# Average pooling on one core: stores of two tiles in one 4 MiB DMA, the first one held back

## The chip, the cores and the metric

One core of one Trainium2 chip. The time is device microseconds (us) of that core; lower is better.

## The reference

```python
def setup_inputs():
    return {"x": np.random.randn(64, 256, 8192).astype(np.float32),
            "kernel_size": 4, "stride": 4}

def reference(x, kernel_size, stride):
    # output[:, :, i] = mean(x[:, :, 4*i : 4*i+4]), shape (64, 256, 2048)
    ...
```

Each output is the mean of four neighbours. 536.87 MB are read, 134.22 MB written, and every output costs three additions and one multiplication. Moving the data is the work.

## The kernel before

The 64 x 256 = 16384 rows are cut into 64 tiles of 256 rows: 128 partitions with two rows each. A tile's load is 8 MiB, 64 KiB of contiguous HBM in each partition; its store is 2 MiB, 16 KiB in each partition. There are two input buffers (`_NIN`) and four output buffers (`_NOUT`). The SP queue loads, DVE adds neighbours in two passes (8.7 and 4.4 us), ACT multiplies by 1/4 (3.6 us) and issues the store. A load waits until the second pass on the tile two before it is done.

```python
_NIN, _NOUT = 2, 4
U, E = _NOUT, NT // _NOUT - 1            # NT = 64 tiles

def load(h, u, r0=0, r1=R, wait=True):
    b = u % _NIN
    if wait:
        nc.sync.wait_ge(s_dve, h * U + (u - _NIN + 1))
    nc.sync.dma_start(
        out=xin[:, b * T + r0 * L : b * T + r1 * L],
        in_=xg[:, h * U + u, r0 * L : r1 * L],
    ).then_inc(s_last if r0 > 0 else s_in[b], 16)

def add_up(h, u, r0=0, r1=R):            # on DVE
    ...                                  # waits: output buffer stored, tile landed
    pairs(half, src).then_inc(s_half, 1)
    ...
    pairs(obuf(u, r0, r1), half).then_inc(s_dve, 1)

# ... ACT, the steady loop:
with nc.scalar.Fori(0, E) as h:
    for u in range(1, U + 1):
        v = u % U
        nc.scalar.wait_ge(s_dve, h * U + (u + 1))
        nc.scalar.mul(obuf(v), obuf(v), inv_k).then_inc(s_act, 1)
        nc.scalar.wait_ge(s_act, h * U + (u + 1))
        nc.scalar.dma_start(out=og[:, h * U + u, :], in_=obuf(v)).then_inc(s_out[v], 16)
# ... the last tiles are stored from the SP queue, the very last in two halves
```

## Time and profile before

| | before |
|---|---|
| time, median of the 3 runs given with it | 1554.84 us (1554.72 to 1555.09) |
| span in the profile | 1553.0 us |
| moved | 671.1 MB, 432 GB/s over the span |
| DMA engines' time in packets | 80.8% + 19.2% = 100% |
| DVE, ACT busy | 54%, 15% |
| period of a tile in the middle | 24.18 us |

The page of the kernel before. Its queue lines give packets, megabytes and the share of 16 engines' span that the packets took (q1 is the SP queue, with all loads and the last stores; q10 is the ACT queue, with the other stores). The group line of DVE ends with the idle time before it and what ended it. The issue lines give KB of one DMA and the median time from issue to landing.

```profile
span 1553.0 us, 976 instructions
...
DMA packets 18720, 671.10 MB, mean 432 GB/s; under 512 B 2080, under 2 KB 2080, under 8 KB 2080
...
q1 hardware_dynamic: 9936, 543.17, 80.8%
q10 hardware_dynamic: 8784, 127.93, 19.2%
...
L85 DVE TENSOR_TENSOR xin<-xin 128x8192 f32<-128x8192 f32 (+1 forms) x65 | 556.5, 8561 | 702.3 <-DMA xin<-in_x_dram 702.3
...
out_dram<-res ACTq DMA_DIRECT2D x61, 2048.0 KB, 52.4
...
xin<-in_x_dram SPq DMA_DIRECT2D x63, 35.0
```

The two shares add up to the whole span: apart from about 2 us at the start and 1.5 us at the end, no engine of the 16 has free time. (Recorded durations overlap by 3 to 4 ns from one packet to the next, 2418 ns recorded against 2414 from start to start, which is why the sum reaches 100% in spite of the two ends.) DVE waits 702 us for loads and for nothing else. A store lands 52.4 us after its issue although a new one is issued every 24.2 us, so there is always a second store queued behind the one in progress.

The windows view of two tile periods (columns: the stretch, its length, busy time of DVE, ACT and POOL, the granted clock, the DMA share, GB/s):

```profile
300.00:348.36 48.36, 26.23 (x4) 7.23 (x2) 0.00 (x0) 1.00 1.00 434
```

Two tiles are 20 MiB; 20 MiB in 48.36 us is 434 GB/s at a DMA share of 1.00. The Trainium skill ("DMA: Bandwidth & Descriptors", section "Where 436 GB/s comes from") puts the ceiling of a core's DMA fabric at 435 GB/s; this trace agrees, and loads and stores share it. The same section expects transfers between HBM and SBUF to be held to about 358 GB/s by the HBM side; with one core at work that was not so here, and the measured 434 GB/s decides.

The packet records of one engine, listed from the trace (time, queue, bytes, recorded duration in ns; records of 4 bytes are a DMA's completion). The engine's identity is not recorded: this is one chain in which each record starts where another ends. First the middle of the run, then the first store of the run:

```
400082  q10  16384   611          53612  q1   65536  2418
400689  q1       4     9          56026  q1   65536  2441
400695  q10  16384   611          58464  q1   65536  3249   <- slow
401302  q1   65536  2418          61710  q10  16384   611   <- first store
403716  q10  16384   611          62317  q1       4     9
404323  q1   65536  2418          62323  q10  16384   611
406738  q10  16384   611          62930  q1   65536  2418
```

Left: strict turns between the two queues, and a completion record uses a turn, though it takes only 6 ns. Right: beside the first store a load packet takes 0.83 us longer than the usual 2.418. Added over all 16 engines and divided by 16, this is the **excess**: 0.89 us between 50 and 95 us, and 0.00 from 100 us to the end. Only records that are more than 12 ns over the usual duration of their size are counted.

### The profile page before, as it was taken

To read this page: it belongs to the slowest core of one execution; us is meant where nothing else is said; L and a number is where in the kernel's file an instruction comes from. 1 tells how busy PE (TensorE), PEld (TensorE's weight loads), DVE (VectorE), ACT (ScalarE), POOL (GpSimd) and SP (SyncE) were. 2 spreads that over 40 slices of the span, in tenths; PEclk is the share of its full clock that TensorE was granted. 3 is DMA by queue.
4 is the path that set the end of the run, shared out by engine and by line. 5 is a ranking of instruction groups with operands and counts; after the bars stand their busy time and mean duration, and the time that the engine had idled before them with its cause. 6 is when DMAs were issued, how large, how long until landed. Compare 5 with 4: busy or idle time off the path is not lost.

```text
span 1553.0 us, 976 instructions
## 1 busy us (share of the span) xinstructions
DVE 839.8 (54%) x130; ACT 232.9 (15%) x66; POOL 0.2 (0%) x4
## 2 busy tenths in 40 slices
DVE  3645546456465564654646546455464554645546
ACT  1111011110111101101011010110101101111011
POOL 0000000000000000000000000000000000000000
DMA  9999999999999999999999999999999999999999
GB/s 405 425 433 439 439 439 436 415 439 432 439 439 439 432 417 434 439 439 432 442 415 433 438 432 446 439 420 428 434 440 439 439 432 418 433 439 439 439 425 405
DMA packets 18720, 671.10 MB, mean 432 GB/s; under 512 B 2080, under 2 KB 2080, under 8 KB 2080
## 3 DMA queue, kind: packets, MB, share of 16 engines
q1 hardware_dynamic: 9936, 543.17, 80.8%
q10 hardware_dynamic: 8784, 127.93, 19.2%
HBM read 536.87 MB, written 134.22 MB: 432 GB/s over the span
## 4 chain that ended last, share of the span: by engine, by line
DMA 72%; DVE 27%; issue 0%; SPq 0%; ACT 0%; DVEq 0%
DMA xin<-in_x_dram 72%; DVE xin L85 18%; DVE res L85 9%; SPq L68 0%; ACT res L106 0%; DVEq L96 0%; SPq L188 0%; SPq L57 0%
## 5 line engine op out<-in xcount | busy, mean ns | idle before, releaser
L85 DVE TENSOR_TENSOR xin<-xin 128x8192 f32<-128x8192 f32 (+1 forms) x65 | 556.5, 8561 | 702.3 <-DMA xin<-in_x_dram 702.3
L141 ACT ACTIVATE res<-res 128x4096 f32<-128x4096 f32 x60 | 217.0, 3616 | 1225.8 <-DVE res L85 1225.8
L85 DVE TENSOR_TENSOR res<-xin 128x4096 f32<-128x4096 f32 (+1 forms) x65 | 283.4, 4359 | 2.2
L106 ACT ACTIVATE res<-res 128x4096 f32<-128x4096 f32 (+1 forms) x5 | 14.7, 2933 | 86.6 <-DVE res L85 86.6
L106 ACT ACT_TABLE_LOAD x1 | 1.3, 1283 | 0.9 <-SPq L57 0.9
L174 POOL MEMSET const-bfloat16-1.0<- 128x1 bf16 x1 | 0.1, 101 | 0.0
L174 POOL MEMSET const-uint8-127<- 128x1 uint8 x1 | 0.1, 101 | 0.0
L174 POOL MEMSET const-float32-0.0<- 128x1 f32 x1 | 0.1, 98 | 0.2 <-issue 0.2
L174 POOL MEMSET const-float32-1.0<- 128x1 f32 x1 | 0.1, 98 | 0.0
## 6 DMA issues: line engine op xcount, KB each, us to landing
out_dram<-res ACTq DMA_DIRECT2D x61, 2048.0 KB, 52.4
xin<-in_x_dram SPq DMA_DIRECT2D x2, 4096.0 KB, 29.5
out_dram<-res SPq DMA_DIRECT2D x2, 2048.0 KB, 26.1
out_dram<-res SPq DMA_DIRECT2D x2, 1024.0 KB, 9.4
xin<-in_x_dram SPq DMA_DIRECT2D x63, 35.0
```

Source lines behind the costliest of these rows:

```text
L85: return nc.vector.tensor_tensor(out=out, in0=v[:, :, 0], in1=v[:, :, 1], op=mybir.AluOpType.add)
L106: nc.scalar.mul(o, o, inv_k).then_inc(s_act, 1)
L141: nc.scalar.mul(obuf(v), obuf(v), inv_k).then_inc(s_act, 1)
L174: nc = _bacc.Bacc("TRN2", target_bir_lowering=False, num_devices=1)
```

## The change

The intent, as stated: one 4 MiB store for every two tiles, still in 16 KiB packets, so that half as many stores are issued; the first store is held until the third tile has landed, so that the next one is queued in time. The output memory stays the same: two buffers of two tiles instead of four of one.

```diff
+_G = 2
-_NOUT = 4
+_NOUT = 2
+    og2 = of.rearrange("(g t p r) m -> p g t (r m)", t=G, p=P, r=R)
-    res = pool.tile([P, _NOUT * OT], dt)
+    res = pool.tile([P, _NOUT * G * OT], dt)
@@ the store
-            eng.dma_start(
-                out=og[:, h * U + u, : r1 * OL], in_=obuf(u, 0, r1)
-            ).then_inc(s_out[u], 16)
+            eng.dma_start(
+                out=og2[:, h * _NOUT + u // G, :, :],
+                in_=res[:, (u + 1 - G) * OT : (u + 1) * OT].rearrange(
+                    "p (t m) -> p t m", t=G
+                ),
+            ).then_inc(s_out[u // G], 16)
@@ DVE waits for a stored output buffer after its first pass, not before it
-                nc.vector.wait_ge(s_out[u], h * 16)
             pairs(half, src).then_inc(s_half, 1)
+            if u % G == 0:
+                nc.vector.wait_ge(s_out[u // G], h * 16)
@@ ACT: the hold, and a store after every second tile
-        scale(0, 0)
-        nc.scalar.wait_ge(s_dve, 2)
-        store(nc.scalar, 0, 0)
+        for u in range(G):
+            scale(0, u)
+        nc.scalar.wait_ge(s_in[0], 32)
+        store(nc.scalar, 0, G - 1)
     # (the steady loop issues one store where u % G == G - 1;
     #  the last stores, 4 + 2 + 1 + 1 MiB, go out from the SP queue. Cut.)
```

More of the change, by code (lines that the diff above doesn't have):

```diff
@@ L36 @@
     R = _R
+    G = _G
     T, OT = R * L, R * OL
-    assert OL * K == L and rows % (P * R * _NOUT) == 0
+    assert OL * K == L and rows % (P * R * G * _NOUT) == 0
     NT = rows // (P * R)
@@ L57 @@
     with tc.tile_critical():
-        U = _NOUT
+        U = _NOUT * G
         E = NT // U - 1
@@ L74, in obuf, with store, store_rows @@
             return res[:, u * OT + r0 * OL : u * OT + r1 * OL]
-        def store(eng, h, u, r1=R):
-            eng.wait_ge(s_act, h * U + (u + (1 if r1 == R else r1)))
+        def store(eng, h, u):
+            eng.wait_ge(s_act, h * U + (u + 1))
             eng.dma_start(
-                out=og[:, h * U + u, : r1 * OL], in_=obuf(u, 0, r1)
-            ).then_inc(s_out[u], 16)
+                out=og2[:, h * _NOUT + u // G, :, :],
[3 more added lines that the diff above has]
+            ).then_inc(s_out[u // G], 16)
+        def store_rows(eng, u, r1, scaled):
+            eng.wait_ge(s_act, scaled)
+            eng.dma_start(
+                out=og[:, E * U + u, : r1 * OL], in_=obuf(u, 0, r1)
+            ).then_inc(s_in[0], 16)
         def pairs(out, src):
@@ L118 @@
             load(E, U - 1, r, r + 1, wait=r == 0)
-        for u in range(1, U - 1):
-            store(nc.sync, E, u)
-        store(nc.sync, E, U - 1, R - 1)
+        store(nc.sync, E, G - 1)
+        store_rows(nc.sync, U - 2, R, NT - 1)
+        store_rows(nc.sync, U - 1, R - 1, NT - 1 + R - 1)
         with nc.vector.Fori(0, E) as h:
@@ L130 @@
             add_up(E, U - 1, r, r + 1)
-        scale(0, 0)
-        nc.scalar.wait_ge(s_dve, 2)
-        store(nc.scalar, 0, 0)
-        with nc.scalar.Fori(0, E) as h:
-            for u in range(1, U + 1):
+        for u in range(G):
+            scale(0, u)
+        nc.scalar.wait_ge(s_in[0], 32)
+        store(nc.scalar, 0, G - 1)
+        with nc.scalar.Fori(0, E - 1) as h:
+            for u in range(G, U + G):
                 v = u % U
@@ L141 @@
                 nc.scalar.mul(obuf(v), obuf(v), inv_k).then_inc(s_act, 1)
-                nc.scalar.wait_ge(s_act, h * U + (u + 1))
-                nc.scalar.dma_start(out=og[:, h * U + u, :], in_=obuf(v)).then_inc(
-                    s_out[v], 16
-                )
-        scale(E, 1)
-        scale(E, 2)
-        scale(E, 3, 0, 1)
-        scale(E, 3, 1, 2)
-        nc.sync.wait_ge(s_out[0], E * 16 + 16)
+                if u % G == G - 1:
+                    nc.scalar.wait_ge(s_act, h * U + (u + 1))
+                    nc.scalar.dma_start(
+                        out=og2[:, h * _NOUT + u // G, :, :],
+                        in_=res[:, (v + 1 - G) * OT : (v + 1) * OT].rearrange(
+                            "p (t m) -> p t m", t=G
+                        ),
+                    ).then_inc(s_out[v // G], 16)
+        for u in range(G, U):
+            scale(E - 1, u)
+        store(nc.scalar, E - 1, U - 1)
+        for u in range(U - 1):
+            scale(E, u)
+        for r in range(R):
+            scale(E, U - 1, r, r + 1)
+        nc.sync.wait_ge(s_out[1], E * 16)
     nc.sync.dma_start(
-        out=og[:, NT - 1, (R - 1) * OL :], in_=res[:, _NOUT * OT - OL :]
+        out=og[:, NT - 1, (R - 1) * OL :], in_=res[:, _NOUT * G * OT - OL :]
     )
```

## The prediction

> **What bounds the kernel now.** The DMA engines: the page's queue table gives 80.8% + 19.2% = 100% of 16 engines' span; 671.1 MB in 1553.0 us is 432 GB/s. DVE is busy 54%, ACT 15%. The windows view of two tiles (100 to 148.36 us) gives DMA share 1.00. In the packet records an engine passes a 64 KiB load packet every 2.414 us when loads run alone, and a load packet plus a 16 KiB store packet every 3.022 us when both queues have work: alternating costs nothing. Eight such pairs and two completion records (6 ns each) make a tile's 24.18 us. All engines are idle only for some 2 us at the start and 1.5 at the end. So at most about 3 us (0.2%) can be won.
>
> **What the change does.** Bytes, packet sizes (stores were in 16 KiB packets already), loads, DVE and ACT work stay. About 32 completion records per engine go: 0.2 us. The last DVE, ACT and store steps stay hidden behind queued stores. Issues (0.34 us on ACT) are off the path. In work alone the change is worth 0 to 0.3 us.
>
> **The queue's turns.** In the records each engine alternates strictly between load and store queue, and a completion record takes a turn like a packet. (The Trainium skill, "DMA: Bandwidth & Descriptors", section "Queues, rings and completion order", says that each engine round-robins between queues at packet granularity; this trace agrees.) Before, a tile takes 8+1 load turns and a store 8+1: balanced, so the store queue, once filled, never empties. After, two tiles take 18 load turns, one 4 MiB store 16+1 = 17: the store queue runs ahead by one turn, about 2.2 us, per pair. A store is ready about 19 us after its second tile lands (DVE 8.7+4.4, ACT 3.6, issue, start-up). Holding the first store gives the second about 5 us of margin; after three or four stores it is used up, and from then on the store queue empties before each next store, some 26 times.
>
> An empty store queue alone costs nothing, since loads fill the time. But the one time that stores started beside running loads in the before kernel (about 58 us), the packets then in flight took 3.2 to 3.4 us instead of 2.42 on all 16 engines: 0.9 us lost. If each restart costs that, 26 x 0.9 = 23 us: about 1578. If it is paid only the first time, about 1554.7. I hold the recurring stall for somewhat more likely (about 60%), given that the queue empties at all (about 85%).
>
> **Prediction.** 1570 us, between the two outcomes and nearer the slower; 8 in 10 between 1553.5 and 1581. Faster by over 2%: 1%. Within 2%: 95%. Slower by over 2%: 4%.
>
> **What would show it.** A period of 48.36 us per two tiles: no stall; near 49.3, with 64 KiB packets of about 3.3 us once per two tiles: the stall recurs. The store queue's packets should pause once per store from about the fifth store on. DVE waits for loads alone; a wait on output buffers before its second addition would be new and is not expected (about 19 us of margin). Last load to end: 14 to 20 us, without idle engines.
>
> **What would make it wrong.** A 4 MiB store's completion taking more turns, so that the queue never empties (1554.7); a stall of another size; rows 2 MiB apart per partition written slower than 0.607 us a packet; an idle end, if the last stores queue worse than worked out.

## The result, and the profile after

| | before | after |
|---|---|---|
| time, median of 4 runs | 1554.91 us | 1554.91 us |
| range | 1554.72 to 1555.09 | 1554.75 to 1555.18 |
| ratio, 95% interval | | 1.0000 (0.9983 to 1.0018) |
| span | 1553.0 us | 1553.0 us |
| last packet ends | 1551.8 us | 1551.7 us |
| completion records per engine | 130 | 99 |

Ratios, here and below, are the mean time of one kernel's fast runs over that of the other's of the same rounds, so not quite the ratio of the medians that are quoted.

The page of the kernel after; the lines answer to those of before:

```profile
span 1553.0 us, 843 instructions
...
DMA packets 18224, 671.09 MB, mean 432 GB/s; under 512 B 1584, under 2 KB 1584, under 8 KB 1584
...
q1 hardware_dynamic: 10064, 545.26, 81.1%
q10 hardware_dynamic: 8160, 125.83, 18.9%
...
L100 DVE TENSOR_TENSOR xin<-xin 128x8192 f32<-128x8192 f32 (+1 forms) x65 | 556.4, 8561 | 697.8 <-DMA xin<-in_x_dram 697.8
...
out_dram<-res ACTq DMA_DIRECT2D x30, 4096.0 KB, 49.5
...
xin<-in_x_dram SPq DMA_DIRECT2D x63, 35.0
```

The same shares, the same waits of DVE. The packet count fell by 496 = 31 x 16 completion records. At about 5.8 ns each that is 31 x 5.8 ns = 0.18 us per engine, which is all that the change removes. The windows view of the same stretch after the change:

```profile
300.00:348.36 48.36, 26.23 (x4) 7.23 (x2) 0.00 (x0) 1.00 1.00 434
```

The line is the same to the last digit. The store queue, however, does what the prediction worked out. One engine's records around the end of one store and the start of the next, after the change:

```
295472  q10  16384   611
296079  q1   65536  2418
298498  q10      4     9   <- end of a store: the store queue is empty
298503  q1   65536  2418
300918  q1   65536  2418
303332  q10  16384   611   <- the next store, 4.8 us later
303939  q1       4     9
303945  q10  16384   611
304552  q1   65536  2418   <- no slow packet
```

Of the 4.8 us, 2.4 us are the load packet whose turn it is in any case (the kernel before shows 2.4 us at every store); the second load packet shows that the store queue was empty. The first such gap stands before the fifth store; from there to the last store of the ACT queue it comes 26 times. Between 100 us and the end the excess is 0.00 us. The excess of the run's first store is still there: 0.89 us between 50 and 95 us. So the queue empties as predicted, and no cost of a restart can be seen in these records.

### The profile page after: what moved, and what is told of

Its sections match the earlier page's. It is cut to its first block, busy times and chain, and to the rows that moved or that the text cites. A ratio compares the mean times of both kernels' runs of the same rounds, so it can differ in the third digit from the quotient of the medians.

```text
span 1553.0 us, 843 instructions
## 1 busy us (share of the span) xinstructions
DVE 839.6 (54%) x130; ACT 232.9 (15%) x66; POOL 0.2 (0%) x4
## 4 chain that ended last, share of the span: by engine, by line
DMA 71%; DVE 28%; issue 0%; SPq 0%; ACT 0%; DVEq 0%
DMA xin<-in_x_dram 71%; DVE xin L100 18%; DVE res L100 9%; SPq L73 0%; ACT res L122 0%; DVEq L116 0%; SPq L212 0%; SPq L62 0%
## 5 line engine op out<-in xcount | busy, mean ns | idle before, releaser
L158 ACT ACTIVATE res<-res 128x4096 f32<-128x4096 f32 x56 | 202.5, 3616 | 1149.0 <-DVE res L100 1149.0
L122 ACT ACTIVATE res<-res 128x4096 f32<-128x4096 f32 (+1 forms) x9 | 29.1, 3237 | 159.0 <-DVE res L100 159.0
```

What stands on the lines that cost most here:

```text
L122: nc.scalar.mul(o, o, inv_k).then_inc(s_act, 1)
```

## The experiments

Eleven runs, on four chips; each is compared with the kernel before on its own chip (medians 1554.88 to 1554.95). All results were correct. In what follows *excess* is as defined above, and *gap* is the time for which an engine has no store while loads go on.

### 1. Without the hold

```diff
-        nc.scalar.wait_ge(s_in[0], 32)
```

> The change without its hold: the first 4 MiB store goes out as soon as its two tiles are scaled (about 59 us instead of 61.5). Theory A (the 16 DMA engines are saturated and a restart of the empty store queue costs nothing, so the order of packets does not matter): within 0.5 us of 1554.9; turn count 17 against 18 makes the store queue run dry from about the third store on instead of the fourth or fifth, with the same gap of about 4.8 us before each later store; the one slow spell of the load packets at the first store (0.9 us per engine in both kernels) stays once. Theory B (restarts cost, and the hold is what saves the change from them): more restarts with a cost, 1 to 25 us slower.

Measured: 1555.13 us against 1554.95, ratio 1.0001 (0.9987 to 1.0014). Excess 0.79 us at the first store, 0.01 from 100 to 1500 us. One expectation was missed: in the mean of the 16 engines the first gap of over 4 us stands before the fifth store, as it does with the hold, and not earlier; there are 26 in both. So the margin that the hold was to give the second store cannot be seen in the gaps. The hold is worth nothing that these runs can see, and theory B falls.

### 2. A longer hold

```diff
-        nc.scalar.wait_ge(s_in[0], 32)
+        nc.scalar.wait_ge(s_in[1], 32)
```

> The change with the first store held one tile longer, until the fourth tile has landed. The third pair's output buffer is then still being stored when DVE wants to write it: one new DVE wait of about 17 us for the store, at tile 4. Theory A: the engines still always have a packet from one queue or the other, so 1554.9 within 0.5 us in spite of the wait. Theory B (a compute wait of 17 us delays the next load and is lost): about 1560 to 1572.

Measured: 1556.45 us, ratio 1.0009 (0.9994 to 1.0024); 1.5 us over the median of before, with no overlap of the runs (1555.73 to 1557.05), though the interval does not exclude 1. The new wait, in the view of waits (who waited on what; total us, times, longest):

```profile
DVE res L100 <- DMA out_dram<-res: 16.4, 1, 16.4
```

The wait came as expected, once, 16.4 us; nine tenths of it were hidden. The 1.5 us that were not hidden match the excess from 100 to 1500 us: 1.46 us, in this run alone of the first two. It lies in two places. While DVE waits, the next load is not issued, and the load queue runs dry. When it starts again (139 us) its packets take a little longer; about 15 us later, when the next store starts, two load packets take 2.88 and 3.01 us. So the slow packets of the first store came a second time here, but not at the 26 restarts of the change. This was the lead for experiments 5 to 9.

### 3. The kernel before with halved loads: many restarts

```diff
+            mid = (r0 + r1) * L // 2
+            for c0, c1 in ((r0 * L, mid), (mid, r1 * L)):
-            nc.sync.dma_start( ... r0 * L : r1 * L ... ).then_inc(..., 16)
+                nc.sync.dma_start( ... c0 : c1 ... ).then_inc(..., 16)
     # (the thresholds of the waits for loads are doubled)
```

> The kernel before with every load cut into two DMAs of 32 KiB packets, so that a tile takes 16+2 load turns against 9 store turns: the store queue must run dry before each of some 60 stores, for about 11 us each. Twice the number of restarts of the change, with longer gaps, nothing else moved. Theory A: a restart costs nothing; what is added is the smaller packets alone, 16 x 64 x (1.2095 - 1.207) us = 2.6 us, and 64 completion records of 6 ns = 0.4 us: about 1557.9. The prediction's theory (0.9 us for each restart): 60 x 0.9 us more, about 1612. A store should land about 27 us after its issue instead of 52.

Measured: 1559.40 us, ratio 1.0028 (1.0015 to 1.0042). The prediction's theory wanted 1612. 58 gaps of about 10.9 us, read from the packet records; excess from 100 to 1500 us 0.02 us. The issue line shows that a store no longer has another queued before it:

```profile
out_dram<-res ACTq DMA_DIRECT2D x61, 2048.0 KB, 18.5
```

18.5 us from issue to landing instead of 52.4 (27 were expected). The time is 1.5 us above theory A's sum; of this 0.85 us is idle engine time at the very end (1.15 us against 0.30 in the last 5 us before the last packet). The rest is in the records too: load and store packets that are longer by a few ns each, below the 12 ns of the excess, add up to 0.7 us from 100 to 1500 us. Even if all of it were put down to the 58 restarts, it would be 13 ns for each; 58 of them at 0.9 us would have shown 52 us.

### 4. The change with 8 KiB packets: the store queue falls behind

```diff
+                    for r in range(R):
                     nc.scalar.dma_start(
-                        out=og2[:, h * _NOUT + u // G, :, :],
+                        out=og2[:, h * _NOUT + u // G, :, r * OL : (r + 1) * OL],
                         ...
     # (two DMAs of 2 MiB for each pair of tiles; the thresholds of s_out are doubled)
```

> The change with each 4 MiB store as two 2 MiB stores in 8 KiB packets: 34 store turns against 18 load turns in two tiles. Now the store queue falls behind, output buffers are not free in time, and DVE should wait for stores about 15 to 30 times, 200 us or more in all (none in the change). Theory A: the engines stay busy with stores while loads are held up, so only the cost of the smaller packets is added, about 64 x 8 x 3.5 ns = 1.8 us and 32 more completion records: 1556.5 to 1557.5. Theory B (waits of DVE for buffers delay loads and leave the engines without work): 10 us or more above that.

Measured: 1582.94 us, ratio 1.0181 (1.0167 to 1.0195). The turn count was right: DVE waits for stores 15 times, 220.9 us in all.

```profile
DVE res L101 <- DMA out_dram<-res: 220.9, 15, 15.7
```

Theory A was wrong here by 26 us. The packets themselves add 2.2 us to the change (records times their usual duration). The rest is excess, 16.9 us from 100 to 1500 us and 1.8 after, and idle engines, 4.4 us from 100 to 1500 us and 3.5 more in the last 5 us than before. Each DVE wait holds back a load, the load queue runs dry, and the stores that are queued then do not always last until the load has started. One engine's records in such a place: stores alone until 724.0 us, then eight load packets alone, of 3.05 us (the first) and 2.99 us (the last, when stores start again), with smaller delays in between. The sentence "the engines always have a packet from one queue or the other, so nothing is lost" is thus not enough.

### 5. A tiny early write

```diff
+        nc.vector.memset(tiny[:, :], 0.0).then_inc(s_m, 1)         # on DVE, first
+        nc.scalar.wait_ge(s_m, 1)
+        nc.scalar.dma_start(out=og[:, 0, :128], in_=tiny[:, :]).then_inc(s_w, 16)
         scale(0, 0)
         nc.scalar.wait_ge(s_dve, 2)
+        nc.scalar.wait_ge(s_w, 16)
```

> The kernel before with one extra tiny write on the store queue (128 x 512 B of zeros into rows that the first store overwrites later) issued about 1 us after the start. It asks what the 0.9 us at the first real store is. Theory Cold (the first DMA of a queue, or its first write, is slow once): the load packets at 55 to 62 us keep 2.42 us, and the excess of 0.9 us is gone there. Theory Gap (a store queue that stood empty for long, here over 50 us with loads alone, costs about 0.9 us when it starts again): the excess of 0.9 us stays at 55 to 62 us. Theory Load start (the first mixing after the load queue itself was started from empty costs it): it moves to the tiny write at the start. Time within 1 us of 1554.9 in all three; the packet records decide.

Measured: 1555.73 us, ratio 1.0004 (0.9987 to 1.0021). The excess stays where it was: 1.08 us between 50 and 95 us. So it is not a cost of the first DMA of a queue or of its first write. The tiny packets (27 ns each) did take turns with load packets from 7.4 us on, and this did not pay it either. Of the three theories this result fits Gap alone; experiments 6 and 7 test Gap.

### 6 and 7. The change with halved and quartered loads: long gaps

```diff
+            w = (r1 - r0) * L // 2          # 4 in the other kernel
+            for c0 in range(r0 * L, r1 * L, w):
-            nc.sync.dma_start( ... r0 * L : r1 * L ... ).then_inc(..., 16)
+                nc.sync.dma_start( ... c0 : c0 + w ... ).then_inc(..., 16)
     # (thresholds of the waits for loads times 2, or 4)
```

> The change with every load cut into two DMAs of 32 KiB packets. The load queue has 36 turns in two tiles against 17 of a store, so the store queue should stand empty for about 20 us before each of about 30 stores (4.8 us in the change, 10.9 us in the kernel before with halved loads), and loads never run dry. Theory Gap: a restart after 17 us or more of loads alone costs 0.9 to 1.0 us, as it did once in the run with the longer hold: 30 x 0.95 = 28 us above the 1559.4 of the kernel before with halved loads, about 1588. Theory Load start (it costs only after the load queue too was empty): about 1559.4 within 1 us.

> The change with every load cut into four DMAs of 16 KiB packets: the store queue stands empty for about 29 us before each of about 30 stores. Smaller packets add 64 x 8 x (4 x 607.1 - 2414.3) ns = 7.2 us and 192 completion records 1.2 us: about 1564 by Theory Load start; 28 us more, about 1592, by Theory Gap.

Measured: 1559.39 us (ratio 1.0028) and 1569.88 us (1.0096, 1.0079 to 1.0113). The gaps are 21.8 and 30.5 us, once per store. Excess from 100 to 1500 us: 0.01 and 0.06 us. Theory Gap falls: it wanted 1588 and 1592. With quartered loads the time is 6 us over the sum, without a slow spell: the 16 KiB load packets took 613.2 ns in the mean instead of 611.0, which makes 4.4 us for the 2016 packets of an engine. The small lengthenings do not lie at the restarts: from 100 to 1500 us, 3.9 of 4.2 us fall on load packets with no store on any engine within 1.5 us (3.0 ns each in the mean, 0.5 ns for those with a store near). With halved loads it is 0.8 of 0.9 us. Why small load packets take longer alone is open. Another 1.4 us of the 6 is idle time at the end (1.75 us in the last 5 us before the last packet, against 0.30).

### 8. A full early store, twice

```diff
+        nc.vector.memset(obuf(3), 0.0).then_inc(s_m, 1)             # on DVE, first
+        nc.vector.wait_ge(s_w, 16)      # first kernel: before tile 0; second: before tile 3 alone
+        nc.scalar.wait_ge(s_m, 1)
+        nc.scalar.dma_start(out=og[:, 0, :], in_=obuf(3)).then_inc(s_w, 16)
         scale(0, 0)
         nc.scalar.wait_ge(s_dve, 2)
+        nc.scalar.wait_ge(s_w, 16)
```

> The kernel before with one extra full store of 2 MiB (zeros, in 16 KiB packets, into rows that the first store overwrites later) at about 6 us, while the first loads run; then the store queue stands empty until the first real store at about 60 us. The extra bytes cost 2 MiB / 433.7 GB/s = 4.85 us: about 1559.8. If the 0.9 us spell is paid once after the load queue has been started, at the first stores of full size, its excess appears at 6 to 10 us and the packets at 55 to 65 us keep 2.42 us. If it belongs to the first real store or to a store queue that stood empty, it stays at 55 to 65 us, or comes twice (about 1560.7).

Measured: 1562.69 us, ratio 1.0052 (1.0036 to 1.0069). This run was badly made: the extra wait kept DVE from the first tile until the early store had landed, the third load was issued late, and the load queue ran dry at 47 us. Excess 0.69 us at 5 to 30 us, then 0.63 at the restart of the loads, and 1.11 at 50 to 95 us. It came twice, but so did the start of the load queue. The mended run:

> The run with an early full store again, mended: DVE now waits for that store only at the fourth tile, so that the loads do not run dry at 47 us as they did there. Expected 1554.9 + 4.85 = 1559.8 us. If the slow spell is paid once per start of the load queue, when packets of a full store first mix with it, the excess of about 0.9 us lies at 5 to 30 us and there is none at 60 to 70 us. If it stays at 60 to 70 us, the first mixing does not pay it and that reading falls.

Measured: 1560.37 us, ratio 1.0036 (1.0019 to 1.0053). Excess 0.87 us at 5 to 30 us and **0.00 us at 50 to 95 us**, although the store queue then stood empty for 34 us before the first real store. One engine's records, left the early store, right the first real one:

```
  7627  q1   65536  2587          61518  q1   65536  2418
 10210  q10  16384   611          63932  q1   65536  2418
 10817  q1   65536  2418          66346  q10  16384   611   <- first real store
   ...                            66953  q1       4     9
 22906  q1   65536  2979          66959  q10  16384   611
 25882  q10  16384   611          67566  q1   65536  2418   <- no slow packet
```

So here the spell is paid once, while the early full store mixes with a load queue that has been started, and the later restart of the store queue is free. Two things limit this. The 0.87 us have two parts: 0.3 us at 6 to 9 us, where stores join, and 0.55 us at 21 to 24 us, after some five pairs of packets (the 2979 above); what parts them is not shown. And this run alone would also fit a rival, that the first store of full size in a run is slow; against it stand the runs in which the slow spell came again later, after the load queue had run dry (2, the first run of 8, and 9).

### 9. The load queue let run dry on purpose, in both kernels

```diff
                 nc.sync.wait_ge(s_dve, h * U + (u - _NIN + 1))
+                if u == _NIN:                       # kernel before
+                    nc.sync.wait_ge(s_in[1], h * (U // _NIN * 16) + 16)
+                if u == _NIN + 1:                   # kernel after
+                    nc.sync.wait_ge(s_in[0], h * (U // _NIN * 16) + 32)
```

> The kernel before with one load in four issued only when the load before it has landed, so that the load queue runs dry 16 times for about 2 us each; stores are still queued then and fill most of that time. If a load queue that is started again from empty costs 0.5 to 1.5 us, with slow packets at that load or at the next store: 8 to 24 us more, about 1563 to 1579. If the dry spell costs nothing by itself because the store queue has packets: 1554.9 within 1 us, and then the slow spells of the run with the longer hold and of the run with 8 KiB stores need another cause.

Measured: 1578.34 us (1575.38 to 1580.06), ratio 1.0151 (1.0134 to 1.0168), as the first branch said. The late loads are seen in the waits of the SP queue (total, times, longest), and the loss in the starts of DVE's first pass; every fourth tile is 26.2 us after the one before it, the others about 24.

```profile
SPq L70 <- DMA xin<-in_x_dram: 159.1, 15, 10.9
```

```profile
925.80 8.69 DVE L87 TENSOR_TENSOR xin<-xin 128x8192 f32<-128x8192 f32 x1 [11.09 <-DMA xin<-in_x_dram]
...
952.03 8.69 DVE L87 TENSOR_TENSOR xin<-xin 128x8192 f32<-128x8192 f32 x1 [13.08 <-DMA xin<-in_x_dram]
...
975.68 8.69 DVE L87 TENSOR_TENSOR xin<-xin 128x8192 f32<-128x8192 f32 x1 [10.49 <-DMA xin<-in_x_dram]
...
1024.04 8.69 DVE L87 TENSOR_TENSOR xin<-xin 128x8192 f32<-128x8192 f32 x1 [11.09 <-DMA xin<-in_x_dram]
```

925.80 to 1024.04 is 98.24 us for four tiles, against 2 x 48.36 = 96.72: 1.5 us for each dry spell. Engines were idle for only 0.73 us in all from 100 to 1500 us; the excess there is 16.13 us. The profiled run took 1577.10 us, 22.2 us over the median of before; about 17 us of this lie in that stretch and the rest in the first and last dry spells. One engine's records of that spell:

```
926519  q10  16384   611
927126  q10      4     9
927132  q1   65536  2918   <- loads start again
930046  q1   65536  2665
932707  q1   65536  2418
   ...
942376  q1   65536  2429
944802  q1   65536  3209   <- before the next store
948007  q10  16384   611
```

Half a microsecond or more at the restart, and 0.8 us where the next store starts, 20 us later. In the same kernel two early spells stand apart, and the same engine's records show how:

```
138150  q10  16384   611          239171  q10  16384   611
   ...  (stores alone)               ...  (stores alone)
142405  q10  16384   611          243420  q10      4     9
143012  q1   65536  2459          243426  q1   65536  2418
145468  q10  16384   611             ...  (seven loads alone, not slow)
146075  q1   65536  2418          260325  q10  16384   611
148489  q10  16384   611          260932  q1   65536  2942   <- slow
```

Left, the spell at 138 us: the next store is already queued, stores run on beside the restarted loads, and nothing is slow. Right, the spell at 239 us: the restart itself is not slow and no engine is idle, but the loads run alone for seven packets, and when stores join, the next load packet takes 0.5 us more. From about 530 us on the stores often end before the loads start again, and both parts are paid. So of the 14 spells from 100 to 1500 us one costs nothing, the next three 0.3 to 0.5 us each, and the last ten 1.2 to 1.7 us each.

> The change with one load in four issued only when the load before it has landed: 16 dry spells of about 2 us of the load queue, but at a moment when a 4 MiB store has some 14 of its 16 packets per engine left, so that stores mix with the restarted load at once and the store queue does not stand empty during it. If every start of the load queue from empty costs, whatever the store queue does: 16 x 1.0 to 1.5 us, about 1571 to 1579. If the cost needs a store queue that was empty while the restarted load ran: about 1555 to 1558.

Measured: 1562.45 us (1562.22 to 1562.65), ratio 1.0048 (1.0031 to 1.0065): between the two branches, and the trace says why. The load queue ran dry as often,

```profile
SPq L75 <- DMA xin<-in_x_dram: 160.3, 15, 11.1
```

but from 100 to 1500 us, which holds all but the first and the last dry spell, the excess is 0.57 us and idle time 0.00. Four tiles in the middle:

```profile
597.20 8.69 DVE L102 TENSOR_TENSOR xin<-xin 128x8192 f32<-128x8192 f32 x1 [6.25 <-DMA xin<-in_x_dram]
...
693.99 8.69 DVE L102 TENSOR_TENSOR xin<-xin 128x8192 f32<-128x8192 f32 x1 [6.21 <-DMA xin<-in_x_dram]
```

96.79 us, against 96.72 without dry spells. The 7.5 us of the whole run come from the two ends: the first dry spell fell before any store was queued, the last at the end of the ACT queue's stores; together they hold all of 4.9 us of idle engines and most of the rest of the excess. In the middle nine store packets bridge the dry spell and the restarted loads alternate with stores at once:

```
644365  q10      4     9
644371  q10  16384   611
   ...                      (nine store packets, no load)
649227  q10  16384   611
649834  q1   65536  2418   <- loads start again, not slow
652248  q10  16384   611
652855  q1   65536  2418
```

Every second store of this run also comes after a gap of about 21.7 us, and these restarts are free too. So a dry load queue costs nothing by itself if stores fill the time and go on beside the restarted load. It costs 0.3 to 0.5 us where the restarted loads run alone (six to eight packets in the runs here) and stores join them later, and about 1.5 us where the restart itself is slow too.

### All runs

| run | time (us) | ratio | store restarts, gap | excess 100-1500 us |
|---|---|---|---|---|
| after | 1554.91 | 1.0000 | 26, 4.8 us | 0.00 |
| 1 no hold | 1555.13 | 1.0001 | 26, 4.8 us | 0.01 |
| 2 longer hold | 1556.45 | 1.0009 | loads dry once | 1.46 |
| 3 before, halved loads | 1559.40 | 1.0028 | 58, 10.9 us | 0.02 |
| 4 change, 8 KiB packets | 1582.94 | 1.0181 | loads held back 15 times | 16.89 |
| 5 tiny early write | 1555.73 | 1.0004 | one, after tiny packets, 37 us | 0.01 |
| 6 change, halved loads | 1559.39 | 1.0028 | 29, 21.8 us | 0.01 |
| 7 change, quartered loads | 1569.88 | 1.0096 | 29, 30.5 us | 0.06 |
| 8 full early store | 1562.69 | 1.0052 | loads dry once, at 47 us | 0.00 |
| 8 mended | 1560.37 | 1.0036 | one, 34 us | 0.01 |
| 9 before, dry loads | 1578.34 | 1.0151 | loads dry 16 times, then alone | 16.13 |
| 9 change, dry loads | 1562.45 | 1.0048 | loads dry 16 times, stores beside them | 0.57 |

No run beats either kernel. The records of both sum to 1547.8 and 1547.6 us per engine at their usual durations; what is left of the 1553.0 us span is the start (about 2 us without a packet and 0.6 us of slow first packets), the one excess of 0.9 us, and the end.

## Why the prediction was wrong

- **What bounds the kernel, and what the change is worth in work alone:** right. 100% of the engines' time before and after; 0.18 us of completion records went, the time moved by less than the runs' scatter.
- **The turns:** right. 18 load turns against 17 store turns, the queue runs dry before the fifth store and each later one, 26 times. The margin credited to the hold was not: without it the gaps begin at the same store (run 1). The skill's statement on round-robin ("DMA: Bandwidth & Descriptors", section "Queues, rings and completion order") carried this, with one difference that the trace shows: see the last section.
- **No DVE waits on output buffers, and no idle end:** right. DVE waited for loads alone; the last load packet ended at 1532.2 us, the last packet 19.5 us later, with all engines busy up to the last microsecond or two.
- **The step that failed:** "If each restart costs that, 26 x 0.9 = 23 us", held likely at 60%. One observation, the slow packets at the first store, was read as a property of *starting an empty store queue*, which stood next to it in the records. Restarts of the store queue show an excess of 0.00 to 0.06 us in total in 26, 58, 29 and 29 cases with gaps of 4.8, 10.9, 21.8 and 30.5 us (the small lengthenings of experiments 3, 6 and 7 lie mostly elsewhere). What the slow packets go with in these runs is the other queue: a load queue that was started from empty and ran alone, when stores of full size join it. That condition holds once in either kernel, at the start of the run, so the true size of the term is 1 x 0.9 us in both, and it cancels. The evidence: it moved to 5 to 30 us, and vanished from the first real store, with an early full store (run 8, mended); it came back, up to 1.7 us a spell, when the load queue was let run dry and the restarted loads ran alone (run 9, kernel before), and not when stores ran beside the restarted loads (run 9, kernel after, and the spell at 138 us in the kernel before).
- **The number given:** the measured 1554.91 us is the lower of the two outcomes that were named (1554.7). But 1570, the figure given, stood between two outcomes, neither of which was 1570, and leaned to the wrong one.
- **What stays open:** why a restarted load stream owes this time, and why part of it can fall 12 us after the stores have joined (run 8, mended). No run shows what happens inside an engine. The two runs of experiment 9 differ in more than the point of interest (2 MiB against 4 MiB stores, and which tile's load is late); within one kernel the contrast rests on the few early spells. That the run with 8 KiB packets lost its 26 us in this way is argued from its records, not shown by undoing it.
- **The hold,** which is part of the change's stated intent, guards against something that costs nothing here (run 1); one tile longer, the loads run dry once and the median is 1.5 us higher (run 2; its interval does not exclude 1, but the excess in its trace is 1.46 us).

## What to carry to other kernels

When the DMA engines are full from end to end, count what a change takes from their work: here 31 records of 6 ns; regrouping the same packets into larger DMAs could give no more. Keep the load queue from running dry rather than the store queue from running empty: the first cost up to 1.7 us a time where the restarted loads ran alone, the restarts of the second nothing that could be measured in over 160 cases. Before multiplying a stall that the trace shows once, ask for the second place where its supposed cause also occurs: a run with many restarts, as in experiment 3, would have settled it.

## What the Trainium skill lacked or had wrong

- "DMA: Bandwidth & Descriptors", section "Queues, rings and completion order", says that an engine drains a packet of typically 9 to 17 descriptors before it turns to the next queue. Here it turned after every single packet record of 64 or 16 KiB (the trace does not say how many descriptors a record holds), and a completion record used a turn of its own (6 ns). This, 9 against 9 turns before and 18 against 17 after, decides whether a store queue runs dry; the page does not say it.
- The same page, section "Rules for kernel authors", asks for at least 1 MiB per DMA for bandwidth. The rule has no word on what more brings when the next DMA is already queued or the engines are full: going from 2 to 4 MiB stores gave a ratio of 1.0000 here. The section "Anatomy of one DMA — SWDGE (gpsimd) path" fits about 2 us of fixed cost to a DMA; with the next DMA already queued, one DMA less freed 6 ns of each engine here, the length of its completion record (these are queues of SP and ACT, not of GpSimd).
- No page tells what a load queue costs that has run dry: 0.3 to 1.7 us for a spell when the restarted loads ran alone before stores joined them (13 spells of run 9, kernel before), about 0 when stores ran beside them, and 0.9 us in both kernels where the first stores joined the loads.
